# A matmul with rotary embedding: ten input buffers instead of twenty-four, six output buffers instead of four, and the last pieces handed over smaller

## The chip, the cores and the metric

One core of a Trainium2 chip. The metric is the time of one execution in device microseconds. Times are quoted as medians. A ratio is the mean time of one kernel's fast runs over that of the other kernel's fast runs of the same rounds, so it is not quite the ratio of the medians. A profile's *span* is from the first to the last instruction; in every execution here the time lies 1.8 us above the span.

"Slow" is a label for a run that is over 1.5% above the fastest of the same kernel.

## The reference

```python
def reference(x, weight, cos, sin, n_heads):      # x [16, 512, 768], weight [768, 768], all float32
    # shortened: cos1, cos2, sin1 and sin2 are the halves of cos and sin
    y = np.matmul(x, weight).reshape(batch, seq, n_heads, head_dim)      # 12 heads of 64
    y1, y2 = y[..., :32], y[..., 32:]
    out1 = y1 * cos1 - y2 * sin1                                         # cos, sin: [512, 64]
    out2 = y2 * cos2 + y1 * sin2
    return np.concatenate([out1, out2], axis=-1).reshape(batch, seq, hidden)
```

## The kernel before

The 8192 rows of x are 64 tiles of 128 rows, worked on as 32 pairs. A tile is loaded (SyncE issues the transfer, 384 KB), cast to fp16 by ScalarE, transposed by TensorE (6 transposes), copied out of PSUM by ScalarE, and multiplied by the weight (12 matmuls). VectorE multiplies the pair's result by cos and by the swapped sin, GpSimd adds the two products into an output buffer, and ScalarE's queue issues the store (768 KB for a pair). A copy that follows a store in ScalarE's program waits behind it: in the rows shown below, the store at 56.98 goes out late and the copy comes after it, at 57.40.

```python
AHEAD = 8
xpool = ctx.enter_context(tc.tile_pool(name="xpool", bufs=24))     # tiles of x, fp32
opool = ctx.enter_context(tc.tile_pool(name="opool", bufs=4))      # finished pairs
# ...
def rope_pair(n):
    rope(n, 0, 2 * H, psys[n].rearrange("p b n -> p (b n)"))       # VectorE: two products
    add(n, 0, 2 * H, nc.gpsimd)                                    # GpSimd: their sum
# ...
for n in range(2, NP):
    while loaded < min(NP, n + AHEAD):
        load_plain(loaded)                                         # SyncE
        loaded += 1
    # ...
    for s in (0, 1):
        for c in CHUNKS:
            mm(n, s, *c)
        upto("turn", 2 * n + s + 3)                                # transposes; ScalarE copies them out
        upto("cast", 2 * n + s + 5)                                # ScalarE
        if n >= NP - ALONE:                                        # the last three pairs go tile by tile
            if (n, s) != (NP - 1, 1):
                rope_alone(n, s)
                add(n, s * H, (s + 1) * H, nc.gpsimd)
    if n >= 3:
        store(n - 3, nc.scalar)                                    # ScalarE's queue issues the store
    # ...
    if n < NP - ALONE:
        rope_pair(n)
store(NP - 3, nc.scalar)
store(NP - 2, nc.scalar)
store(NP - 1, nc.scalar, 0, H)
rope_last(NP - 1, 1, (nc.sync, nc.sync))                           # last tile: VectorE alone, two stores
```

Of the kernel before, what the change touches and what calls it, by code (L numbers as in the profile page):

```python
# [12 lines left out]
MULT = mybir.AluOpType.mult  # L13
ADD = mybir.AluOpType.add
# [3 lines left out]
def kernel(  # L18
# [9 lines left out]
    nc = tc.nc  # L28
    P = nc.NUM_PARTITIONS

    B, S, H = x.shape
    NH = int(n_heads)
    D = H // NH
    HD = D // 2
# [3 lines left out]
    SB = S // P  # L38
    NP = B * SB // 2
    CHUNKS = [(t, e) for t in range(NT) for e in range(2)]  # L40
    AHEAD = 8
    AHEAD_B = 4
    ALONE = 3

# [3 lines left out]
    def where(n, s):  # L48
        return 2 * (n // SB) + s, n % SB

    def by_blocks(n, s):
        return False
# [5 lines left out]
    csn = konst.tile([P, 2, SB, D], FP32)  # L58
    w_raw = konst.tile([P, NT, 2, H], FP32)
    w_sb = konst.tile([P, NT, 2, H], FP16)  # L60

    xpool = ctx.enter_context(tc.tile_pool(name="xpool", bufs=24))
    bpool = ctx.enter_context(tc.tile_pool(name="bpool", bufs=AHEAD_B + 1))
    cpool = ctx.enter_context(tc.tile_pool(name="cpool", bufs=6))
    tpool = ctx.enter_context(tc.tile_pool(name="tpool", bufs=9))
    rpool = ctx.enter_context(tc.tile_pool(name="rpool", bufs=3))
    opool = ctx.enter_context(tc.tile_pool(name="opool", bufs=4))
    pt_pool = ctx.enter_context(tc.tile_pool(name="pt", bufs=2, space=bass.MemoryType.PSUM))
    py_pool = ctx.enter_context(tc.tile_pool(name="py", bufs=2, space=bass.MemoryType.PSUM))
    cold_ps = pt_pool.tile([P, 512], FP32, tag="pt", name="cold_ps")  # L70
# [1 line left out]
    xss, x16, xTT, psys, tqs, ovs = {}, {}, {}, {}, {}, {}  # L72
# [7 lines left out]
    def load(n, s):  # L80
        b, r = where(n, s)
        xss[n, s] = xpool.tile([P, H], FP32, tag="xs", name="xs")
        nc.sync.dma_start(  # L83
            out=xss[n, s], in_=x[b].rearrange("(p r) h -> r p h", r=SB)[r]
        )

    def load_plain(n):
        for s in (0, 1):
            if n < NP and not by_blocks(n, s):
                load(n, s)  # L90
# [40 lines left out]
    def transpose_blocks(n, s):  # L131
        xT = tpool.tile([P, NT, P, 2], FP16, tag="xT", name="xT")
        nc.vector.transpose(
            out=xT.bitcast(FP32).rearrange("p t m e -> p (t m e)"),
            in_=x16.pop((n, s)).bitcast(FP32),
        )
        xTT[n, s] = xT.rearrange("p t m e -> p t e m")
# [5 lines left out]
    def psum(n, s):  # L143
        if n < NP - ALONE:
            if n not in psys:
                psys[n] = py_pool.tile([P, 3, 512], FP32, tag="psy", name="psy")
                if n < 2:
                    nc.tensor.matmul(  # L148
                        psys[n][:, 1], cold[:, 0:P], cold, start=True, stop=False
                    )  # L150
            cut = 512 if s == 0 else 256
            return [
                (psys[n][:, s, ds(s * 256, cut)], 0, cut, n < 2 and s == 1),
                (psys[n][:, s + 1, 0 : H - cut], cut, H, n < 2 and s == 0),
            ]
        if (n, s) not in psys:
            if (2 * (n - NP + ALONE) + s) % 3 == 1:
                psys[n, s] = [
                    pt_pool.tile([P, 512], FP32, tag="pt", name="psz") for _ in (0, 1)
                ]  # L160
            else:
                ps = py_pool.tile([P, 3, 512], FP32, tag="psy", name="psy")
                psys[n, s] = [ps[:, 0], ps[:, 1]]
        lo, hi = psys[n, s]
        return [(lo, 0, 512, False), (hi[:, 0 : H - 512], 512, H, False)]

    def mm(n, s, t, e):
        for ps, lo, hi, joined in psum(n, s):
            nc.tensor.matmul(  # L169
                ps,  # L170
                xTT[n, s][:, t, e, :],
                w_sb[:, t, e, lo:hi],
                start=((t, e) == CHUNKS[0] and not joined),
                stop=((t, e) == CHUNKS[-1] and not (joined and s == 0)),
            )

    def rope(n, c0, c1, ps):
        r = n % SB
        nh = (c1 - c0) // D
        if n not in tqs:  # L180
            tqs[n] = rpool.tile([P, 2, 2 * H], FP32, tag="tq", name="tq")
            ovs[n] = opool.tile([P, 2 * H], FP32, tag="ov", name="ov")
        nc.vector.tensor_tensor(  # L183
            out=tqs[n][:, :, c0:c1].rearrange("p j (h d) -> p j h d", d=D),
            in0=ps.rearrange("p (h d) -> p h d", d=D)
            .unsqueeze(1).broadcast_to((P, 2, nh, D)),
            in1=csn[:, :, r, :].unsqueeze(2).broadcast_to((P, 2, nh, D)),
            op=MULT,
        )

    def add(n, c0, c1, eng):
        w = c1 - c0
        tq = tqs[n][:, :, ds(c0, w)]
        eng.tensor_tensor(  # L194
            out=ovs[n][:, ds(c0, w)].rearrange("p (h t d) -> p h t d", t=2, d=HD),
            in0=tq[:, 0].rearrange("p (h t d) -> p h t d", t=2, d=HD),
            in1=tq[:, 1].rearrange("p (h t d) -> p h t d", t=2, d=HD)[:, :, ::-1, :],
            op=ADD,
        )

    def rope_pair(n):
        rope(n, 0, 2 * H, psys[n].rearrange("p b n -> p (b n)"))
        add(n, 0, 2 * H, nc.gpsimd)

    def rope_alone(n, s):
        for ps, lo, hi, _ in psum(n, s):
            rope(n, s * H + lo, s * H + hi, ps)



    def rope_last(n, s, engs):
        r = n % SB
        for (ps, lo, hi, _), eng in zip(psum(n, s), engs):
            nh = (hi - lo) // D
            q = tqs[n][:, 1, ds(s * H + lo, hi - lo)]
            ph = ps.rearrange("p (h d) -> p h d", d=D)
            for o, j in ((q.rearrange("p (h d) -> p h d", d=D), 1), (ph, 0)):
                nc.vector.tensor_tensor(  # L218
                    out=o, in0=ph, op=MULT,
                    in1=csn[:, j, r, :].unsqueeze(1).broadcast_to((P, nh, D)),  # L220
                )
            nc.vector.tensor_tensor(  # L222
                out=ovs[n][:, ds(s * H + lo, hi - lo)].rearrange(
                    "p (h t d) -> p h t d", t=2, d=HD
                ),
                in0=ps.rearrange("p (h t d) -> p h t d", t=2, d=HD),
                in1=q.rearrange("p (h t d) -> p h t d", t=2, d=HD)[:, :, ::-1, :],
                op=ADD,
            )
            store(n, eng, s * H + lo, s * H + hi)  # L230

    def store(n, eng, c0=0, c1=2 * H):
        b, r = where(n, 0)
        dst = out.rearrange("b (p r) h -> r p b h", r=SB)[r, :, b : b + 2]
        src = ovs[n].rearrange("p (b h) -> p b h", b=2)
        if c1 - c0 < 2 * H:
            s = c0 // H
            dst = dst[:, s, c0 - s * H : c1 - s * H]
            src = src[:, s, c0 - s * H : c1 - s * H]
        eng.dma_start(out=dst, in_=src)  # L240
# [15 lines left out]
    nc.sync.dma_start(out=sin_sb, in_=sin.rearrange("(p r) d -> p r d", r=SB))  # L256
    for n in range(2, AHEAD):
        load_plain(n)
# [5 lines left out]
    def upto(what, k):  # L264
        k += min(4, max(0, k - 41) // 4)
        while done[what] < min(k, 2 * NP):
            n, s = divmod(done[what], 2)
            done[what] += 1
            if what == "cast":
                cast(n, s, nc.scalar)  # L270
            elif not by_blocks(n, s):
                transpose(n, s, nc.scalar)
# [13 lines left out]
    for k, c in enumerate(CHUNKS):  # L286
# [8 lines left out]
        out=csn[:, 1, :, HD:D], in0=sin_sb[:, :, 0:HD], scalar1=-1.0  # L295
    )
    rope_pair(0)
    upto("cast", 6)
    mm(1, 0, *CHUNKS[-1])
# [4 lines left out]
    upto("turn", 6)  # L304
    upto("cast", 8)
    rope_pair(1)

    loaded = AHEAD
    for n in range(2, NP):

        while loaded < min(NP, n + AHEAD):
            load_plain(loaded)
            loaded += 1
        if n + 1 < NP and by_blocks(n + 1, 1):
            transpose_blocks(n + 1, 1)
        for s in (0, 1):
            for c in CHUNKS:
                mm(n, s, *c)
            upto("turn", 2 * n + s + 3)
            upto("cast", 2 * n + s + 5)  # L320
            if n >= NP - ALONE:
# [4 lines that stand above are left out]
            store(n - 3, nc.scalar)  # L326
        load_blocks(n + AHEAD_B)
        if n < NP - ALONE:
            rope_pair(n)
    store(NP - 3, nc.scalar)  # L330
    store(NP - 2, nc.scalar)
    store(NP - 1, nc.scalar, 0, H)
    rope_last(NP - 1, 1, (nc.sync, nc.sync))


# [33 lines left out]
```

## Time and profile before

| | kernel before |
|---|---|
| time, median | 169.1 us |
| span of the profiled execution, and its time | 168.5 us, 170.3 us |
| TensorE's last matmul ends | 159.96 us |
| from there to the end of the span | 8.54 us |

The page's engine rows, the chain of waits, the totals of the waits and the tail are shown in the prediction. How to read them: in the row of 40 slices a digit is the busy share of a slice in tenths; in the chain, each row is a start, a duration, and what ended last there; in the totals, "A <- B: t, n, m" says that A's engine stood idle for t us in n places, m at most, until B was done. The releaser in these views is inferred from the semaphore event that came last.

### The profile page before, as it was taken

The page shows a single profiled execution, that of the slowest core. Times are in us where ns is not written, and L with a number is a line of the kernel's source. Part 1 is how long each engine was busy: PE and PEld are TensorE (multiplying, and loading weights), DVE is VectorE, ACT ScalarE, POOL GpSimd, SP SyncE. Part 2 cuts the span into 40 slices and gives each one's busy share as a digit, 9 for nine tenths or more (in the row PEclk, how much of TensorE's full clock was granted, in tenths as well). Part 3 has the DMA queues.
Part 4 walks back from the last instruction along what each step waited for, and adds up shares of the span by engine and source line. Part 5 has one row for each costly group of instructions (what it writes and reads, how often), then busy time and mean ns, then how long its engine had stood idle before and what let it go on. Part 6 is the DMA issues. An engine that isn't in the chain of part 4 may idle for free.

```text
span 168.5 us, 2869 instructions
## 1 busy us (share of the span) xinstructions
PE 154.7 (92%) x1170; PEld 99.1 (59%) x1170; DVE 116.0 (69%) x58; ACT 99.6 (59%) x125; POOL 109.4 (65%) x38
## 2 busy tenths in 40 slices
PE   7799999999999499999999999999999999999900
PEld 2455666666666256666666666676666766665500
DVE  0566976777777707777777777776767676789970
ACT  3523876666773356677666677787898788610000
POOL 0000597739952945749997777777876767679980
PEclk9999999999999969999999999999999999999995
DMA  4999999999999999999999997444433444458666
GB/s 168 365 399 402 398 402 402 405 411 322 416 373 412 411 417 415 411 414 414 415 420 405 397 330 292 191 187 160 157 123 153 164 187 189 187 222 339 256 251 243
DMA packets 19390, 53.18 MB, mean 316 GB/s; under 512 B 1840, under 2 KB 2224, under 8 KB 19376
## 3 DMA queue, kind: packets, MB, share of 16 engines
q1 hardware_dynamic: 10656, 28.19, 43.3%
q10 hardware_dynamic: 8720, 24.81, 37.8%
q8 instruction: 9, 0.15, 0.3%
q14 instruction: 5, 0.04, 0.1%
HBM read 27.82 MB, written 25.17 MB: 314 GB/s over the span
## 4 chain that ended last, share of the span: by engine, by line
PE 66%; DMA 17%; DVE 6%; POOL 3%; ACT 1%; issue 1%; POOLq 1%; SPq 1%; ACTq 0%; DVEq 0%
PE psy L169 55%; PE pt L126 10%; DMA xs<-in_x_dram 7%; DVE tq L183 6%; DMA out_dram<-ov 6%; DMA w_raw<-in_weight_dram 4%; POOL ov L194 3%; POOLq L364 1%; SPq L83 1%; ACT xT L76 1%; ACT xc L76 1%; ACTq L240 0%; POOLq L194 0%; DVEq L183 0%
## 5 line engine op out<-in xcount | busy, mean ns | idle before, releaser
L194 POOL TENSOR_TENSOR ov<-tq 128x1536 f32<-128x1536 f32 (+1 forms) x34 | 109.2, 3220 | 54.1 <-DVE tq L183 36.4
L169 PE MATMUL psy<-w_sb,xT 128*128 128x512 f16 (+1 forms) x744 | 132.3, 328 | 2.6 <-ACT xT L76 2.5
L183 DVE TENSOR_TENSOR tq<-psy,csn 128x3072 f32<-128x3072 f32 (+2 forms) x35 | 102.6, 2945 | 39.2 <-PE psy L169 37.8
L169 PEld LDWEIGHTS <-xT 128*128 128x128 f16 x768 | 73.2, 98 | 46.2 <-ACT xT L76 2.7
L76 ACT COPY xT<-pt 128x768 f16<-128x768 f16 x62 | 49.2, 800 | 40.0 <-PE pt L126 35.4
L76 ACT CAST xc<-xs 128x768 f16<-128x768 f32 x62 | 55.4, 901 | 8.3 <-DMA xs<-in_x_dram 8.2
L126 PEld LDWEIGHTS <-xc 128*128 128x128 f16 x384 | 26.5, 99 | 10.9 <-ACT xc L76 1.9
L126 PE MATMUL pt<-ident,xc 128*128 128x128 f16 x384 | 31.6, 220 | 1.4 <-ACT xT L76 0.5
L244 PE MATMUL cold_ps<-cold 128*128 128x512 f16 x16 | 5.6, 494 | 1.2 <-DVE cold L249 1.2
L110 DVE CAST w_sb<-w_raw 128x768 f16<-128x768 f32 x6 | 3.4, 560 | 2.1 <-DMA w_raw<-in_weight_dram 2.1
L169 PE MATMUL psz<-w_sb,xT 128*128 128x512 f16 (+1 forms) x24 | 4.2, 326 | 0.0
L78 DVE CAST xc<-xs 128x768 f16<-128x768 f32 x2 | 1.9, 948 | 3.1 <-DMA xs<-in_x_dram 3.1
L244 PEld LDWEIGHTS <-cold 128*128 128x128 f16 x16 | 1.8, 123 | 3.3 <-issue 1.9
L183 DVE TENSOR_TENSOR tq<-psz,csn 128x1024 f32<-128x1024 f32 (+1 forms) x4 | 3.6, 948 | 0.0
L78 DVE COPY xT<-pt 128x768 f16<-128x768 f16 x2 | 1.1, 558 | 1.7 <-PE pt L126 1.7
L76 ACT ACT_TABLE_LOAD x1 | 1.3, 1283 | 1.1 <-PEq L350 1.1
L222 DVE TENSOR_TENSOR ov<-psy,tq 128x512 f32<-128x512 f32 (+1 forms) x2 | 1.1, 557 | 0.1
L218 DVE TENSOR_TENSOR psy<-psy,csn 128x512 f32<-128x512 f32 (+1 forms) x2 | 1.1, 556 | 0.0
L218 DVE TENSOR_TENSOR tq<-psy,csn 128x512 f32<-128x512 f32 (+1 forms) x2 | 1.1, 554 | 0.0
L249 DVE MEMSET cold<- 128x256 uint32 x1 | 0.3, 272 | 0.9 <-PEq L350 0.9
L148 PE MATMUL psy<-cold 128*128 128x512 f16 x2 | 0.8, 379 | 0.0
L293 DVE COPY csn<-sin_sb 128x128 f32<-128x128 f32 x1 | 0.2, 226 | 0.2 <-DMA sin_sb<-in_sin_dram 0.2
(6 smaller groups left out, 0.8 us busy)
## 6 DMA issues: line engine op xcount, KB each, us to landing
xs<-in_x_dram SPq DMA_DIRECT2D x64, 384.0 KB, 8.4
out_dram<-ov ACTq DMA_DIRECT2D x31, 768.0 KB, 5.6
w_raw<-in_weight_dram SPq DMA_DIRECT2D x6, 384.0 KB, 7.4
out_dram<-ov ACTq DMA_DIRECT2D x1, 384.0 KB, 3.6
out_dram<-ov SPq DMA_DIRECT2D x1, 256.0 KB, 2.3
csn<-in_cos_dram SPq DMA_DIRECT2D x1, 128.0 KB, 7.9
sin_sb<-in_sin_dram SPq DMA_DIRECT2D x1, 128.0 KB, 6.5
out_dram<-ov SPq DMA_DIRECT2D x1, 128.0 KB, 3.4
```

What stands on the lines that cost most here:

```text
L76: eng.copy(out=o, in_=i_)
L78: eng.tensor_copy(out=o, in_=i_)
L83: nc.sync.dma_start(out=xss[n, s], in_=x[b].rearrange("(p r) h -> r p h", r=SB)[r])
L110: nc.vector.tensor_copy(out=w_sb[:, t, e], in_=w_raw[:, t, e])
L126: nc.tensor.transpose(pt[:, t, e, :], xc[:, t, e, :], ident)
L169: nc.tensor.matmul(ps, xTT[n, s][:, t, e, :], w_sb[:, t, e, lo:hi], start=((t, e) == CHUNKS[0] and not joined), stop=((t, e) == CHUNKS[-1] ...
L183: nc.vector.tensor_tensor(out=tqs[n][:, :, c0:c1].rearrange("p j (h d) -> p j h d", d=D), in0=ps.rearrange("p (h d) -> p h d", d=D) .unsqu ...
L194: eng.tensor_tensor(out=ovs[n][:, ds(c0, w)].rearrange("p (h t d) -> p h t d", t=2, d=HD), in0=tq[:, 0].rearrange("p (h t d) -> p h t d", ...
L218: nc.vector.tensor_tensor(out=o, in0=ph, op=MULT, in1=csn[:, j, r, :].unsqueeze(1).broadcast_to((P, nh, D)),)
L222: nc.vector.tensor_tensor(out=ovs[n][:, ds(s * H + lo, hi - lo)].rearrange("p (h t d) -> p h t d", t=2, d=HD), in0=ps.rearrange("p (h t d) ...
L244: nc.tensor.matmul(cold_ps, cold[:, 0:P], cold, start=True, stop=True)
L364: with _tile.TileContext(nc) as tc:
```

## The change

Its intent: in the trace of the kernel before, stores take up to 9.63 us to land while loads are queued and a median of 3.6 after 120 us, so hold the loads to ten tiles; give the stores more time with two more output buffers; let GpSimd start earlier on the last pieces, and shorten VectorE's last work.

```diff
-    AHEAD = 8
+    AHEAD = 7
-    xpool = ctx.enter_context(tc.tile_pool(name="xpool", bufs=24))
+    xpool = ctx.enter_context(tc.tile_pool(name="xpool", bufs=10))
-    opool = ctx.enter_context(tc.tile_pool(name="opool", bufs=4))
+    opool = ctx.enter_context(tc.tile_pool(name="opool", bufs=6))
-    def rope_pair(n):
-        rope(n, 0, 2 * H, psys[n].rearrange("p b n -> p (b n)"))
-        add(n, 0, 2 * H, nc.gpsimd)
+    def rope_pair(n, step=2 * H):
+        ps = psys[n].rearrange("p b n -> p (b n)")
+        for c in range(0, 2 * H, step):
+            rope(n, c, c + step, ps[:, ds(c, step)])
+            add(n, c, c + step, nc.gpsimd)
 # ... rope_last: 512 of the last tile's columns as before, on VectorE;
 #     the other 256 first, their sum on GpSimd, their store from ScalarE's queue
+        rope(n, c1, c2, pz)
+        add(n, c1, c2, nc.gpsimd)
 # ...
-    loaded = AHEAD
-        while loaded < min(NP, n + AHEAD):
-            load_plain(loaded)
-            loaded += 1
+        load_plain(n + AHEAD - 2)
 # ...
-            rope_pair(n)
+            rope_pair(n, 2 * H if n < NP - ALONE - 1 else H)
```

More of the change, by code (lines that the diff above doesn't have):

```diff
@@ L207, in rope_alone, with rope_last @@
             rope(n, s * H + lo, s * H + hi, ps)
-    def rope_last(n, s, engs):
-        r = n % SB
-        for (ps, lo, hi, _), eng in zip(psum(n, s), engs):
-            nh = (hi - lo) // D
-            q = tqs[n][:, 1, ds(s * H + lo, hi - lo)]
-            ph = ps.rearrange("p (h d) -> p h d", d=D)
-            for o, j in ((q.rearrange("p (h d) -> p h d", d=D), 1), (ph, 0)):
-                nc.vector.tensor_tensor(
-                    out=o, in0=ph, op=MULT,
-                    in1=csn[:, j, r, :].unsqueeze(1).broadcast_to((P, nh, D)),
-                )
-            nc.vector.tensor_tensor(
-                out=ovs[n][:, ds(s * H + lo, hi - lo)].rearrange(
-                    "p (h t d) -> p h t d", t=2, d=HD
-                ),
-                in0=ps.rearrange("p (h t d) -> p h t d", t=2, d=HD),
-                in1=q.rearrange("p (h t d) -> p h t d", t=2, d=HD)[:, :, ::-1, :],
-                op=ADD,
-            )
-            store(n, eng, s * H + lo, s * H + hi)
+    def rope_last(n, s):
+        (ps, _, cut, _), (pz, _, _, _) = psum(n, s)
+        c0, c1, c2 = s * H, s * H + cut, (s + 1) * H
+        rope(n, c1, c2, pz)
+        add(n, c1, c2, nc.gpsimd)
+        nh = cut // D
+        q = tqs[n][:, 1, c0:c1]
+        ph = ps.rearrange("p (h d) -> p h d", d=D)
+        for o, j in ((q.rearrange("p (h d) -> p h d", d=D), 1), (ph, 0)):
+            nc.vector.tensor_tensor(
+                out=o, in0=ph, op=MULT,
+                in1=csn[:, j, n % SB, :].unsqueeze(1).broadcast_to((P, nh, D)),
+            )
+        nc.vector.tensor_tensor(
+            out=ovs[n][:, c0:c1].rearrange("p (h t d) -> p h t d", t=2, d=HD),
+            in0=ps.rearrange("p (h t d) -> p h t d", t=2, d=HD),
+            in1=q.rearrange("p (h t d) -> p h t d", t=2, d=HD)[:, :, ::-1, :],
+            op=ADD,
+        )
+        store(n, nc.sync, c0, c1)
+        store(n, nc.scalar, c1, c2)
     def store(n, eng, c0=0, c1=2 * H):
@@ L332 @@
     store(NP - 1, nc.scalar, 0, H)
-    rope_last(NP - 1, 1, (nc.sync, nc.sync))
+    rope_last(NP - 1, 1)
 _INS = ['x', 'weight', 'cos', 'sin', 'n_heads']
```

## The prediction

> **What bounds the kernel now.** I read the page's engine row and 40 slices first, then the chain of waits in order of time, then the waits in total, then the tail in the timeline and in stretches of half a microsecond.
>
> The page says TensorE is busy for 92% of the span, and that the DMA engines are full in the first half and about 40% busy in the second:
>
> ```profile
> PE 154.7 (92%) x1170; PEld 99.1 (59%) x1170; DVE 116.0 (69%) x58; ACT 99.6 (59%) x125; POOL 109.4 (65%) x38
> PE   7799999999999499999999999999999999999900
> DMA  4999999999999999999999997444433444458666
> ```
>
> The one digit 4 in the PE row is the only hole between the start and the tail. The chain in order of time shows what made it:
>
> ```profile
> 35.18 1.95 PE psy L169 x12
> 37.13 0.35 PE pt L126 x6
> 37.51 0.55 ACT xT L76
> 38.06 5.96 DMA xs<-in_x_dram
> 44.09 9.63 DMA out_dram<-ov
> 53.76 0.09 issue
> 53.86 3.45 POOL ov L194
> 57.40 0.81 ACT xT L76
> 58.25 3.40 PE psy L169 x12
> 61.65 0.64 PE pt L126 x6
> 62.29 2.04 PE psy L169 x12
> 64.33 0.34 PE pt L126 x6
> 64.67 1.95 PE psy L169 x12
> ```
>
> A regular tile costs TensorE 1.95 + 0.335 = 2.285 us (12 matmuls, 6 transposes). An output store took 9.63 us, GpSimd could not write its next output buffer until it landed, ScalarE stood at the head of its queue with a store that waited for GpSimd, and so its next copy of transposed x came late and TensorE stood still. The waits in total name the same links:
>
> ```profile
> POOL ov L194 <- DMA out_dram<-ov: 17.7, 10, 5.1
> ACT xT L76 <- POOL ov L194: 4.6, 1, 4.6
> PE psy L169 <- ACT xT L76: 2.5, 1, 2.5
> ```
>
> Size of the hole: in the timeline the tile before it starts at 53.30 and the first regular one after it at 64.50. These are three tiles, 11.20 us, where 3 x 2.285 = 6.86 would do: 4.34 us lost, of which some 2.6 are standing still and 1.7 are slow matmuls after it (3.40 and 2.04 for 1.95, transposes 0.64 for 0.34). From tile 3 (16.90 us) to tile 58 (148.10 us) 55 tiles take 131.2 us; 55 x 2.285 plus the transposes of four tiles done early (1.3) is 127.0. The difference, 4.2, is this hole: nothing else in the steady part is lost.
>
> The tail: TensorE ends at 159.96 and the span is 168.5.
>
> ```profile
> 146.91 3.45 POOL L194 TENSOR_TENSOR ov<-tq 128x1536 f32<-128x1536 f32 x1 [1.44 <-DVE tq L183]
> 151.47 12.30 POOL L194 TENSOR_TENSOR ov<-tq 128x1536 f32<-128x1536 f32 x6 [1.12 <-DVE tq L183]
> 162.05 1.47 SPq L240 DMA_DIRECT2D out_dram<-ov  x2
> 162.50:163.00 0.50, 0.00 (x0) 0.00 (x0) 0.47 (x2) 0.00 (x0) 0.50 (x1) 1.00 0.19 74
> 163.00:163.50 0.50, 0.00 (x0) 0.00 (x0) 0.15 (x1) 0.00 (x0) 0.50 (x1) 1.00 1.03 393
> 166.50:167.00 0.50, 0.00 (x0) 0.00 (x0) 0.00 (x0) 0.00 (x0) 0.00 (x0) 0.50 0.89 332
> ```
>
> The 12.30 us are one run of GpSimd without a gap: the pair (3.45) and five halves of 1.77. It ends at 163.77. The last four stores (768 + 256 + 384 + 128 KB = 1.57 MB) go out between 162.9 and 166.95 at some 390 GB/s: after 162.9 the end is set by bytes, and the bytes start when GpSimd has finished the last whole pair (about 162.0).
>
> [...] stores take up to 9.63 us while loads are queued, and a median of 3.6 to landing after 120 us, when no loads are left. [...] granted clock 0.60 from 58.2 to 61.7, 0.89 to 64.5, then 1.00. [...] GpSimd's pair takes 3.44 to 3.48 us everywhere[...].
>
> **Part 1, loads gated to ten buffers.** The first 14 x tiles are loaded as before: buffers are free, or were freed by the casts of tiles 0 to 3, done by 8.8 us, while these loads are paced to 14 us and later by the eight in flight. From tile 14 on, load k waits for the cast of tile k-10. Casts come every 2.285 us, so loads take 0.393 MB / 2.285 = 172 GB/s, stores the same, together 344 GB/s against some 410 that the page shows when full. No queue builds up. Does a load come in time? Its issue follows the cast ten tiles earlier, so it has 10 x 2.285 - 0.9 = 22 us; the slowest in the trace took 11.2. The order of instructions also shows each store waiting for a load on its own completion semaphore. Store n is then some 12 us later than the issue of that load; with 4 to 8 us to landing this wait is empty. Cost 0.
>
> **Part 2, six output buffers.** GpSimd's pair k starts near 17.8 + 4.57 k, store k is issued near 28.5 + 4.57 k. With four buffers a store has 4 x 4.57 - 10.7 = 7.5 us to land, and 9.6 is too long; with six it has 16.7. The wait of GpSimd for stores (17.7 us) goes to 0, and with it ScalarE's 4.6 and the hole with its cold clock. Gain on the path 4.34 (parts 1 and 2 together; by this sum either would do alone).
>
> **Part 3, last pair of the steady part in halves.** VectorE: by the rows of 512 (681 ns) and 1024 (1215 ns), 1536 elements take 1.75 us; two are 3.50 for 3.36, +0.14. It had 0.26 us of waiting for TensorE before 158.23, so this costs nothing at the end, and the freed PSUM buffer is needed only at 152.00. GpSimd: the first half is ready at 149.8 instead of 151.4, but GpSimd is busy with pair 27 until 150.36. So the backlog starts at 150.38 rather than 151.47, with seven pieces of 1.77: the last whole pair is done at 161.0 (162.0), the half tile at 162.8 (163.77). Gain 1.0.
>
> **Part 4, a third of the last tile to GpSimd.** VectorE's last three 256-column operations (0.41 + 0.42 + 0.42) give way to one product of 0.68, placed first: the 512-column store is issued near 162.65 instead of 162.05. GpSimd adds one piece of 256: from 1813 ns at 768 and 3463 at 1536 about 0.71, so it ends at 163.5. All four stores are then issued by 163.5, and the bytes start at 161.9: 1.57 MB at 390 GB/s end at 165.95 instead of 166.95. Gain of parts 3 and 4 together 1.0; the later 512-column store is hidden behind the 768 KB before it.
>
> Sum: 4.34 + 1.0 = 5.3 us; 169.1 - 5.3 = 163.8 us.
>
> **Rivals.** (a) The gate starves the casts: a wait of ScalarE for x takes the place of its wait for GpSimd. Against it: 22 us of lead, and load bandwidth to spare. For it: combined traffic now lasts the whole kernel at 84% of the full rate, with single transfers up to 11 us. If it came at one place, one more hole of 2 to 4 us: 166 to 168. (b) A store is held by its semaphore's earlier load on ScalarE's in-order queue; margin 12 us minus landing. If this happened each iteration it would cost up to 1 us somewhere, 165. (c) The tail gains nothing, because the small last store (128 KB at 163.5, 3.4 us to landing before) ends as late as now: 164.8. (d) Only the standing still goes, and a shorter wait still lets the clock fall: 165.5. Against it: a full 9 us of slack more.
>
> **Range and chances.** The hole has one cause with large slack on two sides, so I give its removal nine in ten. The tail is between 0 and 1.2. That makes 163.6 to 164.8 if the hole goes; I predict 163.9, range 163.2 to 165.0. Two per cent is 165.7: faster 0.93, same 0.06, slower 0.01.
>
> **What would show it.** No digit below 9 in the PE row between slices 3 and 37; granted clock 1.00 from 58 to 65; no row of GpSimd waiting for the output DMA and none of ScalarE waiting for GpSimd; DMA near 340 GB/s from 30 us to about 125; TensorE's last matmul ending near 155.6; GpSimd's last run without gap from about 146.0 to 159.1; bytes ending some 6 us after TensorE where it was 7.0. A new row of ScalarE waiting for x would make the prediction wrong, as would a PE row that shows a hole elsewhere.

## The result, and the profile after

| | before | changed |
|---|---|---|
| time, median | 169.12 us (168.88 to 170.31, 4 runs) | 165.12 us (164.99 to 165.21, 4 runs) |
| span of the profiled execution | 168.5 us | 163.3 us |
| TensorE's last matmul ends | 159.96 us | 155.62 us |
| from there to the end | 8.54 us | 7.68 us |

The ratio is 0.975 (95% interval 0.970 to 0.980): faster by over 2%. The spans differ by 5.2 us, of which 4.34 in the steady part and 0.86 in the tail. The times differ by only 4.0.

The page's rows of 40 slices of the changed kernel (TensorE, then the DMA engines):

```profile
PE   7899999999999999999999999999999999999910
DMA  4999999998999999999999999989999544459766
```

The hole is gone, and the loads are spread over three quarters of the span instead of three fifths. The chain of waits runs through TensorE alone where the hole was:

```profile
53.47 1.95 PE psy L169 x12
55.42 0.34 PE pt L126 x6
55.76 1.95 PE psy L169 x12
57.70 0.34 PE pt L126 x6
58.04 1.95 PE psy L169 x12
```

Its waits in total:

```profile
POOL ov L194 <- DVE tq L183: 48.6, 27, 18.4
ACT xT L76 <- PE pt L126: 36.1, 53, 1.5
ACT xc L76 <- DMA xs<-in_x_dram: 7.9, 2, 5.0
```

GpSimd waits for VectorE only, no longer for stores; ScalarE waits for TensorE, and for x in two places at the start only (7.9 us, 5.0 at most; the kernel before has 8.2 in three, 5.2 at most). Everything looks as predicted. But the same result would follow from another cause, and the timeline of the kernel before holds a contradiction that I had missed. GpSimd around the hole:

```profile
38.13 6.89 POOL L194 TENSOR_TENSOR ov<-tq 128x1536 f32<-128x1536 f32 x2 [3.13 <-DMA out_dram<-ov]
53.86 3.44 POOL L194 TENSOR_TENSOR ov<-tq 128x1536 f32<-128x1536 f32 x1 [5.14 <-DMA out_dram<-ov]
```

And ScalarE with its queue:

```profile
51.91 0.90 ACT L76 CAST xc<-xs 128x768 f16<-128x768 f32 x1
56.98 0.38 ACTq L240 DMA_DIRECT2D out_dram<-ov  x1
57.40 0.80 ACT L76 COPY xT<-pt 128x768 f16<-128x768 f16 x1 [4.58 <-POOL ov L194]
```

Count the pairs. GpSimd's row at 38.13 is pairs 4 and 5, done at 45.02; the row at 53.86 is pair 7, done at 57.30. Counting the stores on ScalarE's queue from the first at 28.51, the one at 56.98 is store 5. Its data had been ready for 12 us, and it was issued before pair 7 was done. So it did not wait for GpSimd, although the view names GpSimd as the releaser of the copy behind it.

What did store 5 wait for? The packed trace keeps each instruction's semaphores. ScalarE's record just before store 5 is a wait for semaphore 99, which ends at 56.94. The store itself waits for semaphore 110, which only GpSimd's sums update, and its own landing is counted on 99. In each of the two traces the 107 transfers count their landings on the same eight semaphores, 13 or 14 each, and not one of the 99 that have a predecessor on theirs goes out before that predecessor has landed: the closest follows it by 0.015 us. In the kernel before, store 5's predecessor on semaphore 99 is the load of tile 35, twelve pairs ahead. In the changed kernel (semaphore 107) it is the load of tile 25: with ten buffers a load waits for a cast, so fewer loads come between two stores in the order in which the eight semaphores are used (two between stores 4 and 5, five in the kernel before). In the kernel before, the load of tile 35 lands at 56.90 and store 5 goes out at 56.98; stores 3 to 9 all go out 0.07 to 0.08 us after their predecessor, a load each time, has landed. In its second profile a load lands at 60.97 and store 6 goes out at 61.05. In the changed kernel the predecessor had landed at least 1.6 us before the store in every case (6.9 us for store 5). In the same place of the changed kernel, ScalarE goes on without a pause:

```profile
51.22 0.80 ACT L76 COPY xT<-pt 128x768 f16<-128x768 f16 x1 [0.70 <-PE pt L126]
51.28 0.38 ACTq L243 DMA_DIRECT2D out_dram<-ov  x1
51.92 0.91 ACT L76 CAST xc<-xs 128x768 f16<-128x768 f32 x1
53.51 0.80 ACT L76 COPY xT<-pt 128x768 f16<-128x768 f16 x1 [0.68 <-PE pt L126]
```

Three theories were therefore open. A, the prediction's: output buffers come free too late, GpSimd is late, ScalarE's store waits for it. B: ScalarE is held by a store whose completion semaphore belongs to a load far ahead, still in the backlog. C: the load backlog itself, by taking bandwidth.

### The profile page after: what moved, and what is told of

Its sections match the earlier page's. It is cut to its first block, busy times and chain, and to the rows that moved or that the text cites. A ratio compares the mean times of both kernels' runs of the same rounds, so it can differ in the third digit from the quotient of the medians.

```text
span 163.3 us, 2892 instructions
## 1 busy us (share of the span) xinstructions
PE 153.3 (94%) x1170; PEld 98.7 (60%) x1170; DVE 115.5 (71%) x57; ACT 99.6 (61%) x125; POOL 110.3 (68%) x40
## 4 chain that ended last, share of the span: by engine, by line
PE 78%; DMA 8%; DVE 6%; issue 1%; POOLq 1%; SPq 1%; POOL 1%; ACT 1%; DVEq 0%
PE psy L169 66%; PE pt L126 12%; DVE tq L183 6%; DMA xs<-in_x_dram 4%; DMA w_raw<-in_weight_dram 4%; POOLq L363 1%; SPq L83 1%; POOL ov L194 1%; ACT xc L76 1%; POOLq L194 0%; DVEq L183 0%
## 5 line engine op out<-in xcount | busy, mean ns | idle before, releaser
L194 POOL TENSOR_TENSOR ov<-tq 128x1536 f32<-128x1536 f32 (+2 forms) x36 | 110.1, 3068 | 48.6 <-DVE tq L183 48.6
L169 PE MATMUL psy<-w_sb,xT 128*128 128x512 f16 (+1 forms) x744 | 130.8, 326 | 0.0
L183 DVE TENSOR_TENSOR tq<-psy,csn 128x3072 f32<-128x3072 f32 (+3 forms) x37 | 103.4, 2808 | 34.8 <-PE psy L169 34.7
L247 PE MATMUL cold_ps<-cold 128*128 128x512 f16 x16 | 6.2, 535 | 1.2 <-DVE cold L252 1.2
L226 DVE TENSOR_TENSOR ov<-psy,tq 128x512 f32<-128x512 f32 x1 | 0.7, 692 | 0.0
L222 DVE TENSOR_TENSOR psy<-psy,csn 128x512 f32<-128x512 f32 x1 | 0.7, 690 | 0.0
L222 DVE TENSOR_TENSOR tq<-psy,csn 128x512 f32<-128x512 f32 x1 | 0.7, 678 | 0.0
```

The source lines that it names most:

```text
L169: nc.tensor.matmul(ps, xTT[n, s][:, t, e, :], w_sb[:, t, e, lo:hi], start=((t, e) == CHUNKS[0] and not joined), stop=((t, e) == CHUNKS[-1] ...
L183: nc.vector.tensor_tensor(out=tqs[n][:, :, c0:c1].rearrange("p j (h d) -> p j h d", d=D), in0=ps.rearrange("p (h d) -> p h d", d=D) .unsqu ...
L194: eng.tensor_tensor(out=ovs[n][:, ds(c0, w)].rearrange("p (h t d) -> p h t d", t=2, d=HD), in0=tq[:, 0].rearrange("p (h t d) -> p h t d", ...
L222: nc.vector.tensor_tensor(out=o, in0=ph, op=MULT, in1=csn[:, j, n % SB, :].unsqueeze(1).broadcast_to((P, nh, D)),)
L247: nc.tensor.matmul(cold_ps, cold[:, 0:P], cold, start=True, stop=True)
```

## The experiments

All gave correct results. Each kernel was run in turn with the kernel before on the same chip, and the ratios are to those runs. Kernels that are compared with each other by their medians ran in one batch, unless it is said otherwise.

**The kernel before, again (no edit).**

> The kernel before, unchanged, profiled again. The profiled execution of the record had a span of 168.5 us and a time of 170.3, while three other executions took 168.9 to 169.1; the changed kernel's time lies 1.8 us above its span in every execution. Theory A (the hole in the steady part differs from execution to execution, and the recorded profile caught a large one): ratio 1.00, this profile shows a span near 167.3 and a hole of about 3.1 us instead of 4.34. Theory B (the hole is always 4.3 and something else, outside the span, differs): the span is again 168.5 with a hole of 4.3.

Measured: 169.54 us (168.19 to 171.06, 6 runs), ratio 0.997 (0.986 to 1.008). This profile has a span of 166.4 and its hole is in two pieces. TensorE's rows behind them:

```profile
56.44 2.12 PE L169 MATMUL psy<-w_sb,xT 128*128 128x512 f16 x12 [0.55 <-ACT xT L76]
62.32 2.12 PE L169 MATMUL psy<-w_sb,xT 128*128 128x512 f16 x12 [1.14 <-ACT xT L76]
```

No slow matmuls follow: a regular group of 12 is 2.11 long in this view. Measured as in the prediction, from tile 3 to the end of the steady part, this execution loses 2.2 us where the recorded one lost 4.35. Theory A of this run (the hole differs from execution to execution) holds, with a smaller hole than the 3.1 us expected. The 17 runs of the kernel before in these rounds fall into 168.0 to 169.2 and 170.2 to 171.1; the upper ones have mean granted clocks of 0.976 to 0.981, the lower ones 0.982 to 0.989. That fits a hole that is sometimes followed by slow matmuls at a lower clock, as in the recorded profile (granted clock 0.60 from 58.2 to 61.7 us, 0.89 to 64.5), where they cost 1.7 us more. Only one of the 17 was profiled (168.19 us), so for the others this is argued, not shown. The other profiles with the hole agree: slow matmuls in the recorded one (170.3 us; the next 12 take 3.40 us in the chain of waits, where a regular group is 1.95) and with six output buffers (170.28; 3.57 there, granted clock 0.53 from 58.0 to 61.6), none with the tail alone (168.51). But the length of the hole alone did not decide. In that last profile TensorE stood still for 2.93 us, longer than the 2.50 of the recorded one and the 2.8 with six output buffers, and the next tile was regular; why is not shown:

```profile
58.95 2.12 PE L169 MATMUL psy<-w_sb,xT 128*128 128x512 f16 x12 [2.93 <-ACT xT L76]
```

The changed kernel does not show the two groups: its 10 runs lie between 164.84 and 165.61. Seven of the 17 runs carry the label "slow", all of the upper group. That this is the hole and not another state of the chip is likely, not shown; of the 22 runs in the two later batches, one (171.94 us, clock 0.961) lies outside both groups and is unexplained. The label's threshold cuts through the upper group, so a ratio to the kernel before depends on how many runs of each group it holds. The causes below are therefore read from profiles.

**Six output buffers alone.**

```diff
-    opool = ctx.enter_context(tc.tile_pool(name="opool", bufs=4))
+    opool = ctx.enter_context(tc.tile_pool(name="opool", bufs=6))
```

> Six output buffers alone; loads not gated, tail as before. Theory A of the prediction (a store has 16.7 us to land with six buffers, and took 9.6 at worst): no hole, time about 3 to 4 us below before, near 166. Rival (the load backlog is the cause; without the gate the stores queue up and the waits move on to a later buffer or to the casts): the hole stays or moves, 167 to 169.

Measured: 169.19 us, ratio 0.998 (0.990 to 1.007). Theory A is refuted: GpSimd's wait for stores went from 17.7 us to nothing, and the hole stayed at 4.5 us. With GpSimd out of the way the views now name the real releaser. A row of the totals:

```profile
ACT xT L76 <- DMA xs<-in_x_dram: 4.9, 1, 4.9
```

And four of the chain of waits:

```profile
45.64 11.48 DMA xs<-in_x_dram
57.20 0.38 ACTq L240
57.62 0.81 ACT xT L76
58.48 3.57 PE psy L169 x12
```

A load lands at 57.12 after 11.48 us (by the trace it is that of tile 35), and with it ScalarE's store 5 goes out at 57.20, nearly 6 us later than the 51.3 at which the changed kernel issues it. GpSimd had finished that pair at 44.05.

**The gate alone.**

```diff
-    AHEAD = 8
+    AHEAD = 7
-    xpool = ctx.enter_context(tc.tile_pool(name="xpool", bufs=24))
+    xpool = ctx.enter_context(tc.tile_pool(name="xpool", bufs=10))
 # and the loop's load_plain(n + AHEAD - 2)
```

> Loads gated to ten buffers alone; four output buffers, tail as before. By the prediction's sum either part would do alone: with four buffers a store has 7.5 us to land. The changed kernel's stores take a median of 5.8 and up to 8.2 us to landing although gated, so I now expect small waits of GpSimd for stores (a few tenths of a us each) that stay off the path: time about 166. Rival (8.2 over 7.5 is enough to push GpSimd's backlog into ScalarE): a hole of 1 to 3 us, 167 to 168.5.

Measured: 166.12 us, ratio 0.980 (0.974 to 0.987). Its page's row of TensorE:

```profile
PE   7999999999999999999999999999999999999900
```

The steady part is as long as the changed kernel's, within 0.1 us: the gate alone removes the hole, and the two more output buffers bring nothing that can be measured. GpSimd waits 6.1 us in four places for stores, off the path, as I expected. Of the gate, the number of buffers is what acts, by the compiled program's listing and without a run of its own: with ten buffers the listing of SyncE's instructions and their waits is the same with the new loop and AHEAD of 7 as with the old loop and AHEAD of 8, and with twenty-four it is the old one again.

**The stores of the steady part issued from GpSimd's queue.** This keeps the 24 input buffers and the backlog, but takes these stores off ScalarE's queue and, by the compiled program's listing, off the semaphores that they share with loads. It has six output buffers, so the run to compare it with is the one with six output buffers alone.

```diff
-    opool = ctx.enter_context(tc.tile_pool(name="opool", bufs=4))
+    opool = ctx.enter_context(tc.tile_pool(name="opool", bufs=6))
-            store(n - 3, nc.scalar)
+            store(n - 3, nc.gpsimd)
```

> The kernel before with six output buffers, and the stores of the steady part issued from GpSimd's queue instead of ScalarE's: the 24 input buffers and the load backlog stay, but no store stands in ScalarE's in-order queue, and stores no longer share completion semaphores with loads. New theory B (the hole is ScalarE held by a store whose completion semaphore's last user is a load of a tile ten or more pairs ahead, still in the backlog): no wait of ScalarE for x in the steady part, hole gone, TensorE's last matmul near 155.6 and time near 166 (tail as before), unless the issue time on GpSimd makes it late. Theory C (the backlog itself does it, through bandwidth): a hole of 2 to 4 us as before.

Measured: 172.14 us, ratio 1.017 (1.010 to 1.023): slower, but look where. Its stretches of ten microseconds (busy time by engine; the last three columns are granted clock, DMA share and GB/s):

```profile
40.00:50.00 10.00, 10.00 (x79) 6.53 (x77) 7.18 (x3) 7.24 (x10) 8.67 (x6) 1.00 1.02 418
50.00:60.00 10.00, 10.00 (x83) 6.64 (x81) 6.76 (x3) 6.75 (x9) 9.11 (x5) 1.00 1.02 414
60.00:70.00 10.00, 10.00 (x81) 6.55 (x79) 7.58 (x3) 7.03 (x9) 9.13 (x5) 1.00 1.03 415
```

And TensorE's row of the page's 40 slices:

```profile
PE   7799999999999999999999999999999999995000
```

The DMA engines are as full as in the kernel before (shares of 1.02 and 1.03, there 1.01 to 1.03), the stores take longer to land (a median of 6.4 us, there 5.4), and TensorE has no hole; its last matmul ends at 155.48. So here the backlog by itself cost TensorE nothing, and theory C is refuted. What theory B expected of TensorE came true (155.6); the time near 166 us did not. The edit changes the queue and the semaphores at once, and cannot tell one from the other; the landings above do that. The time is lost in the tail: GpSimd issues its stores between the sums (0.73 us each, where ScalarE's rows show 0.38), the last of them goes out at 160.70, 9.5 us before the end of the span, where the last store of the kernel before goes out 4.7 before it, and the span ends 14.8 us after TensorE instead of 8.5.

**Sixteen input buffers.**

```diff
-    xpool = ctx.enter_context(tc.tile_pool(name="xpool", bufs=10))
+    xpool = ctx.enter_context(tc.tile_pool(name="xpool", bufs=16))
```

> The changed kernel with sixteen input buffers instead of ten. By the order of instructions store 5 then waits on the semaphore of the load of tile 31 (35 with twenty-four buffers, 25 with ten), store 3 on that of tile 26 as with twenty-four. Theory B (what matters is how far ahead of its store that load is): store 3 issued about 1.5 us late, all others on time, no hole: within 0.4 us of the changed kernel. Theory C (any backlog of loads costs TensorE time through bandwidth): a hole of 1 to 2 us, 166.5 to 167.

Measured: 165.20 us; the changed kernel took 165.1 and 165.3 in two other batches. Store 3 goes out at 43.66, 1.1 us after its regular place 4.57 us behind store 2, store 5 at 51.59, and no hole follows. Theory B again: what matters here is which load comes before the store on its semaphore (for store 5 that of tile 31, by the listing), not that the gate is tight.

**The tail alone** (pair in halves, third of the last tile on GpSimd; loads and buffers as before).

> The tail alone (last pair in halves, a third of the last tile to GpSimd); loads and buffers as before. Prediction: 1.0 us below before, the hole stays. Rival: the tail gains nothing, since the last small store lands as late as before: same time. Rival 2: the tail gains only as much as the first byte of the last whole pair's store comes earlier.

Measured: 168.67 us, ratio 0.996 (0.988 to 1.004). The hole's scatter hides a gain of 1 us in the times. In the profile the span ends 7.7 us after TensorE instead of 8.5: the tail's gain is 0.9.

**The last pair whole again**, on top of the changed kernel, so that only the third of the last tile is left of the tail's change. It was run beside **the changed kernel again**, the yardstick of these rounds.

```diff
-            rope_pair(n, 2 * H if n < NP - ALONE - 1 else H)
+            rope_pair(n)
```

> The changed kernel once more, as the yardstick for the runs beside it. 165.1 us, all runs within 0.3, span 163.3; no store held on ScalarE.

> The changed kernel with the last pair of the steady part whole again, so that of the tail only the third of the last tile on GpSimd is left. Prediction's sum: GpSimd's run starts 1.0 us later and now carries a piece of 0.7 more, so it ends about 0.7 later than in the kernel before relative to TensorE: 1.0 us slower than the changed kernel, about 166.1. Rival (bytes set the end and the last piece is small): 165.6.

Measured: the yardstick 165.30 us (164.84 to 165.61), ratio 0.976 (0.971 to 0.980); the whole pair 165.98 us, ratio 0.980 (0.976 to 0.984). From TensorE's end to the span's end the whole pair takes 8.7 us (the kernel before 8.5, the yardstick 7.6). So the third alone gains nothing; the halves gain all of it.

**The last tile as before**, on top of the changed kernel.

```diff
-        rope(n, c1, c2, pz)
-        add(n, c1, c2, nc.gpsimd)
 # ... rope_last as in the kernel before: VectorE alone, two stores from SyncE
```

> The changed kernel with the last tile as in the kernel before (VectorE alone, two stores from SyncE); the pair in halves, the gate and six output buffers stay. The run with a whole pair suggests that handing a third of the last tile to GpSimd costs rather than gains: GpSimd then ends at 158.4 instead of 159.1 and VectorE at 158.75. Bytes set the end from 157.5 on, so: as fast as the changed kernel, 165.1 to 165.3 (ratio to it 1.00). Rival (the prediction's part 4: the third is worth a part of the 1.0): 0.3 to 0.6 slower, 165.7.

Measured: 165.04 us (changed kernel in other batches 165.1 and 165.3), and the span ends 7.6 us after TensorE. Handing the third to GpSimd is worth nothing here.

**The store of the last whole pair split in two.** The changed kernel's DMA engines in half microseconds (last two columns: share and GB/s) show an empty stretch after TensorE's end:

```profile
156.00:156.50 0.50, 0.00 (x0) 0.00 (x0) 0.50 (x2) 0.00 (x0) 0.50 (x1) 1.00 0.14 49
157.00:157.50 0.50, 0.00 (x0) 0.00 (x0) 0.50 (x1) 0.00 (x0) 0.50 (x1) 1.00 0.00 0
157.50:158.00 0.50, 0.00 (x0) 0.00 (x0) 0.47 (x2) 0.00 (x0) 0.50 (x1) 1.00 0.85 338
161.50:162.00 0.50, 0.00 (x0) 0.00 (x0) 0.00 (x0) 0.00 (x0) 0.00 (x0) 0.50 0.37 125
```

```diff
-    store(NP - 2, nc.scalar)
+    store(NP - 2, nc.scalar, 0, H)
+    store(NP - 2, nc.scalar, H, 2 * H)
```

> The changed kernel, with the store of the last whole pair (768 KB, issued when GpSimd has done both halves) split into two stores of 384 KB, so that the first fills the 1.5 us in which the DMA engines are idle after TensorE's end. If bytes set the end: 0.9 us faster than the changed kernel, 164.2, then bound by the last piece issued at 159.1. Rival (the last small store's latency sets the end already): no gain.

Measured: 164.62 us beside 165.30, a gain of 0.7 where 0.9 was expected. Now a later half microsecond is empty (158.5 to 159.0), between the last stores (the last goes out at 159.04). That fits an end set by the latest issue and no longer by the bytes; the next run tests it.

**Both: the last tile as before, and the split store**, with the split store alone as yardstick.

> The same with the last whole pair's store split in two. If the third on GpSimd only makes the last store later, this is the fastest so far, 164.3; by the rival it is 165.0.

> The changed kernel with the last whole pair's store split, again, as the yardstick for the runs beside it: 164.6.

Measured: 164.24 us (163.91 to 164.36, ratio to the kernel before 0.968) beside 164.55 (164.49 to 165.07). The former's span ends 6.7 us after TensorE. This is the fastest version that I ran, some 0.5% below the changed kernel (165.1 and 165.3 in other batches). Once the bytes no longer set the end, the third on GpSimd costs 0.3 us: with it the last store goes out 3.5 us after TensorE's end, without it 3.2.

## Why the prediction was right, and where it was wrong

- The direction was right: faster, 0.975. The time was forecast at 163.9 and came to 165.12, just above the top of the range (165.0).
- **What bounds the kernel.** "An output store took 9.63 us, GpSimd could not write its next output buffer until it landed, ScalarE stood at the head of its queue with a store that waited for GpSimd": the last link is wrong. GpSimd did wait for stores, but off the path; six buffers removed that wait and left the hole. ScalarE stood with store 5, which waited on the completion semaphore of the load of tile 35: it landed at 56.90, the store went out at 56.98, and its own data had been ready since 45.02. I took the releaser from the chain without counting which pair the store belonged to.
- **Part 2.** "Gain on the path 4.34 (parts 1 and 2 together; by this sum either would do alone)": the output buffers alone gave 0 (0.998), the gate gave all of it. The forecast of the two together held because the gate was in the change, for a reason that the prediction did not give. That was luck.
- **Part 1 and rival (b).** I looked at the semaphore that a store shares with a load only as a risk of the changed kernel, counted "cost 0", and that was right: no store of the changed kernel was held by a load. I did not put the same question to the kernel before, where it is the cause.
- **Sum.** "169.1 - 5.3" took the hole of one execution from the median of others, whose holes were not profiled. The profiled execution took 170.3 us; from it, 5.3 gives 165.0. The span fell by 5.2 us, almost exactly the sum. The mis-sized term is the hole: 4.34 in the recorded profile, 2.2 in the next of the same kernel.
- **Parts 3 and 4.** The tail's gain of 1.0 was measured as 0.86 by the two recorded profiles. It is all part 3. Part 4 is worth 0 with the stores as they are and costs 0.3 with the split store. That the later 512-column store is hidden behind the bytes of the one before it was right.
- **Rival (a)**, starved casts, did not happen: no new wait for x. **Rival (c)**, no gain in the tail, did not happen either (0.86). **Rival (d)**, a shorter wait that still lets the clock fall, was not seen: the waits of 0.55 and 1.14 us in the second profile of the kernel before were followed by regular tiles (granted clock 1.00 from 50 to 66 us).

## What to carry to other kernels

In this kernel a store waited for a load that had nothing to do with it, because both counted their landings on one semaphore: the load of tile 35 landed at 56.90, store 5 went out at 56.98, and ScalarE, with that store at the head of its queue, stood from 52.81 to 56.98 us. Where a store goes out late, look up what came before it on its semaphore. Before believing a releaser in a profile, count which piece of work the held instruction belongs to, and see whether the named one had long been done. A profile is one execution: subtract what it shows from that execution's own time, and profile a second one where times scatter.
